# The MLP's second layers of chunks 1 to 3 as pairs of seven half products, with weight sums made by accumulating transfers

## The chip, the cores and the metric

The kernel runs on one core of a Trainium2 chip. The metric is the time of one execution in microseconds of device time, given as the median of several runs. A core has five engines that run in parallel, each in its own order: PE (matrix products; its weight loads are listed apart as PEld), DVE (elementwise work on vectors), ACT (activation functions and copies), POOL (a second elementwise engine, which also issues transfers) and SP (issues transfers). Weights and activations lie in SBUF, matrix results in PSUM, which has eight banks. Transfers between HBM and SBUF run on 16 DMA engines.

## The reference, cut to what matters

One layer of a diffusion backbone: two attention mixers, then an MLP with squared ReLU, then a last RMS norm. Width 1024, MLP width 4096, 640 tokens (128 of context, 512 latent).

```python
def _mlp(h, w_mlp_in, w_mlp_out):
    return jnp.square(jax.nn.relu(h @ w_mlp_in)) @ w_mlp_out
...
    h2 = _rmsnorm(x, n2) * (1 + sc2) + sh2
    return x + g2 * _mlp(h2, w1, w2)
...
y_prompt = _rmsnorm(xp, final_norm_g)
y_sample = _rmsnorm(xs, final_norm_g)
```

The scale, shift and gate vectors (`sc2`, `sh2`, `g2`) differ for context and latent tokens.

## The kernel before

Activations are held transposed: a tile has 128 features on the partitions and 640 tokens, in two halves of 320 (`HALVES`; `L0` and `L1` are the same). All values are f32. A product is made of three matmuls: each operand x is split into a high part (ACT rounds it to the matmul's format, fp32r) and a low part (x minus the high part, on DVE or POOL), and high x high, high x low and low x high are summed in PSUM. A full product of one output tile and one half takes 8 slices of depth x 3 = 24 matmuls of 320 columns (`gemm_k`, lines 364 to 370).

The MLP goes in four chunks of 1024 hidden features (the loop at line 1331). Each chunk has a first layer (weights `w1`, input `H2`, the normed residual) and a second (weights `w2`, input the chunk's `hid`), whose result is gated and added into the residual `X1` (`add_gated`, line 1199: one DVE instruction for half 1, two for half 0, since the gate changes at token 128). Chunk 0 is plain: 8 tiles x 2 halves of full products for each layer.

The first layers of chunks 1 to 3 already go by Winograd's form of Strassen's method (`winograd`, line 1306): a pair of output tiles and two halves of the tokens form a 2 x 2 block matrix, and so do the depths (slices 0 to 3 and 4 to 7). Seven half products of 4 slices x 3 = 12 matmuls (`product`, line 1289) replace eight. They need sums of weight blocks (S1 to S4, formed on DVE in `Weights.block`, line 268, recorded at line 278), sums of input blocks (the tiles `T` and the second half of `H2`, formed in `t_pieces`, line 1260, during chunk 0's second layer) and sums of results (DVE adds in `winograd`, line 1311). `relu2` (line 1239) then takes ReLU, square and the high part on ACT, and the low part on DVE. The second layers are full products: 8 tiles x 2 halves x 24 matmuls. The matmuls of pairs are recorded at lines 1293 to 1295, full ones at 368 to 370.

Weights: `Weights` loads tiles of 512 KB through SP into two staging buffers `st` (and two `st2` for the second tile of a pair), converts them (ACT copies the high part, lines 298 and 321; DVE or POOL subtracts for the low part, lines 299, 324 and 326) into six buffers, and converts ahead as these come free. The blocks A12 and A22 have their low part on POOL (`BLKP`), and two of the eight `w2` tiles of a chunk (`W2P`).

PSUM banks rotate through `Units` (seven of the eight); each product or half tile takes the next one. An automatic planner puts each engine's instructions in order and places the waits; it takes the written order as the priority and simulates when each is ready. For DVE alone the written order is kept from line 1128 on (`manual_schedule`). Pieces of other work are hung between products in the list `side`.

In chunk 3 each finished half of `X1` is squared and summed, then scaled by the last norm's gain; after the last half come two matmuls with `ones`, Ln and Exp on ACT, eight products and eight output transfers (`norm_pieces`, `final`).

## Time and profile before

| What | us |
|---|---|
| median of 3 runs | 968.26 (967.52 to 969.08) |
| profiled execution | 968.9 |
| its span, first to last instruction | 967.0 |
| PE busy | 943.8 |
| DVE busy | 647.8 |
| ACT busy | 504.7 |
| POOL busy | 181.0 |

The profile is that of one execution. A busy PE is not PE at its peak, since matmuls are pipelined and one recorded duration (0.309 us) covers more than the distance to the next start. Idle time of an engine that is not the bottleneck costs nothing. Of the 64 weight transfers named `wst<-w` each brings 512 KB. The first layers of chunks 1, 2 and 3 begin at about 640, 746 and 851 us, and the last matmul of chunk 3 starts at 956.80 us; the stretches quoted later follow these borders roughly.

### The profile page before, as it was taken

The page shows a single profiled execution, that of the slowest core. Times are in us where ns is not written, and L with a number is a line of the kernel's source. Part 1 is how long each engine was busy: PE and PEld are TensorE (multiplying, and loading weights), DVE is VectorE, ACT ScalarE, POOL GpSimd, SP SyncE. Part 2 cuts the span into 40 slices and gives each one's busy share as a digit, 9 for nine tenths or more (in the row PEclk, how much of TensorE's full clock was granted, in tenths as well). Part 3 has the DMA queues.
Part 4 walks back from the last instruction along what each step waited for, and adds up shares of the span by engine and source line. Part 5 has one row for each costly group of instructions (what it writes and reads, how often), then busy time and mean ns, then how long its engine had stood idle before and what let it go on. Part 6 is the DMA issues. An engine that isn't in the chain of part 4 may idle for free.

```text
span 967.0 us, 16441 instructions
## 1 busy us (share of the span) xinstructions
PE 943.8 (98%) x6375; PEld 910.2 (94%) x6375; DVE 647.8 (67%) x1336; ACT 504.7 (52%) x1061; POOL 181.0 (19%) x187
## 2 busy tenths in 40 slices
PE   8999899999999999999999999999999999999996
PEld 7799789889999999999999899999999999999995
DVE  4564766755646789698587687688734883478644
ACT  5466667656656754754324653246612762156542
POOL 0362521314321101111123000012201230022100
PEclk9999999999999999999999999999999999999998
DMA  9963310126535346466642063212321233122203
GB/s 344 230 203 110 85 44 25 27 84 150 150 91 153 109 155 218 154 196 199 202 131 88 23 184 122 66 45 88 109 88 39 86 110 94 44 88 66 88 22 109
DMA packets 35774, 111.75 MB, mean 116 GB/s; under 512 B 4672, under 2 KB 8384, under 8 KB 35696
## 3 DMA queue, kind: packets, MB, share of 16 engines
q1 hardware_dynamic: 27408, 83.49, 28.2%
q0 software_dynamic: 7136, 25.90, 9.4%
q10 hardware_dynamic: 1152, 1.31, 0.4%
q8 instruction: 50, 0.82, 0.4%
q14 instruction: 28, 0.23, 0.1%
HBM read 99.40 MB, written 4.60 MB: 108 GB/s over the span
## 4 chain that ended last, share of the span: by engine, by line
PE 85%; DVE 6%; ACT 4%; DMA 2%; issue 2%; POOL 1%; SPq 0%; DVEq 0%; ACTq 0%
PE pg L368 9%; PE pg L369 8%; PE pg L370 8%; PE pss L368 7%; PE pss L370 7%; PE pss L369 7%; PE pt L370 4%; PE pt L368 4%; PE pt L369 4%; PE pss L1293 2%; PE pss L1295 2%; PE pss L1294 2%; DMA ms<-wmodA 2%; PE pt L1293 1%; PE pg L1293 1%
## 5 line engine op out<-in xcount | busy, mean ns | idle before, releaser
L321 ACT ACTIVATE wh<-wst 128x512 fp32r<-128x512 f32 (+1 forms) x115 | 92.3, 822 | 116.4 <-PE pg L369 44.4
L326 DVE TENSOR_TENSOR wl<-wst,wh 128x1024 fp32r<-128x1024 f32 x54 | 66.0, 1222 | 63.5 <-ACT wh L321 63.3
L324 POOL TENSOR_TENSOR wl<-wst,wh 128x512 fp32r<-128x512 f32 (+1 forms) x49 | 76.5, 1575 | 136.1 <-ACT wh L321 119.5
L1083 DVE SCALAR_TENSOR_TENSOR mt<-wmt,cb 128x512 f32<-128x512 f32 x128 | 81.3, 684 | 0.0
L299 POOL TENSOR_TENSOR wb<-wst,wb 128x512 fp32r<-128x512 f32 x24 | 31.7, 1320 | 261.6 <-ACT wb L298 224.9
L644 DVE TENSOR_TENSOR pl<-pt,ph 128x512 fp32r<-128x512 f32 (+2 forms) x80 | 50.8, 635 | 36.3 <-ACT ph L643 31.4
L370 PE MATMUL pss<-hidh,wl 128*128 128x320 f32 x216 | 66.7, 309 | 0.0
L368 PE MATMUL pss<-hidh,wh 128*128 128x320 f32 x216 | 66.7, 309 | 0.0
L369 PE MATMUL pss<-hidl,wh 128*128 128x320 f32 x216 | 66.7, 309 | 0.0
L298 ACT ACTIVATE wb<-sr 128x512 fp32r<-128x512 f32 x48 | 29.8, 626 | 51.2 <-DVE sr L278 39.3
L643 ACT ACTIVATE ph<-pt 128x512 fp32r<-128x512 f32 (+2 forms) x80 | 44.2, 552 | 23.1 <-PE pt L705 10.3
L1252 DVE TENSOR_TENSOR hidl<-rl,hidh 128x320 fp32r<-128x320 f32 x64 | 36.6, 572 | 18.0 <-ACT hidh L1245 17.3
L1079 POOL DMA_DIRECT2D wmt<-wmodB x32 | 17.1, 536 | 165.6 <-DVE mt L1083 108.7
L299 DVE TENSOR_TENSOR wb<-sr,wb 128x512 fp32r<-128x512 f32 x48 | 36.0, 754 | 13.9 <-ACT wb L298 13.8
L368 PE MATMUL pg<-hidh,wh 128*128 128x320 f32 x144 | 44.5, 309 | 0.0
L369 PE MATMUL pg<-hidl,wh 128*128 128x320 f32 x144 | 44.5, 309 | 0.0
L370 PE MATMUL pg<-hidh,wl 128*128 128x320 f32 x144 | 44.5, 309 | 0.0
L368 PE MATMUL pt<-hidh,wh 128*128 128x320 f32 x136 | 42.0, 309 | 0.0
L369 PE MATMUL pt<-hidl,wh 128*128 128x320 f32 x136 | 42.0, 309 | 0.0
L370 PE MATMUL pt<-hidh,wl 128*128 128x320 f32 x136 | 42.0, 309 | 0.0
L370 PEld LDWEIGHTS pss<-hidh,wl 128*128 128x128 f32 x216 | 40.6, 188 | 0.0
L369 PEld LDWEIGHTS pss<-hidl,wh 128*128 128x128 f32 x216 | 40.6, 188 | 0.0
(950 smaller groups left out, 3362.2 us busy)
## 6 DMA issues: line engine op xcount, KB each, us to landing
wst<-w SPq DMA_DIRECT2D x64, 512.0 KB, 3.6
wmt<-wmodB POOLq DMA_DIRECT2D x32, 512.0 KB, 4.4
wst<-w_in SPq DMA_DIRECT2D x31, 512.0 KB, 3.9
ms<-wmodA SPq DMA_DIRECT2D x16, 512.0 KB, 8.0
x<-xT SPq DMA_DIRECT2D x16, 320.0 KB, 6.3
bt<-bias SPq DMA_DIRECT2D x16, 320.0 KB, 5.8
wst<-w_br SPq DMA_DIRECT2D x8, 512.0 KB, 4.5
wst<-w_out SPq DMA_DIRECT2D x8, 512.0 KB, 3.6
```

The costliest lines, as they stand in the source:

```text
L299: later.append(lambda: (nc.gpsimd if name in BLKP else DVE).tensor_sub(t[:, hi4], src, r32(t[:, lo4])))
L321: ACT.activation(hi[:, ks], st[:, ks], AF.Copy)
L324: nc.gpsimd.tensor_sub(lo[:, ks], st[:, ks], r32(hi[:, ks]))
L326: DVE.tensor_sub(lo, st, r32(hi))
L368: PE.matmul(ps, wh[:, k], xh[:, sl], start=first, stop=False)
L369: PE.matmul(ps, wh[:, k], xl[:, sl], start=False, stop=False)
L370: PE.matmul(ps, wl[:, k], xh[:, sl], start=False, stop=last)
L643: ACT.activation(ph[:, :n], pt[:, :n], AF.Copy)
L644: DVE.tensor_sub(pl[:, :n], pt[:, :n], r32(ph[:, :n]))
L1083: DVE.scalar_tensor_tensor(t, st[:, q * 512:(q + 1) * 512], 1.0, r32(cb[2 * q + i][:, :512]), op0=OP.mult, op1=OP.mult, accum_out=parts[:, ...
L1252: DVE.tensor_sub(dst[1][:, sl], r[:, :HT], r32(dst[0][:, sl]))
L1293: PE.matmul(ps, w[:, k], xh, start=k == 0, stop=False)
```

## The change

The second layers of chunks 1 to 3 become pairs of seven half products too. A pair is the output tiles 2n and 2n + 1. For this the host puts the hidden features of these chunks in another order (`w2` in `_host`), so that the first layer's four groups of results are the four blocks of the second layer's input: 11, 12, 21 and 22. `SEQ` lists all products of both layers of the three chunks; the end of a first layer and the begin of its second are interwoven (`FIRST1`, `FIRST2`).

The hidden results stay unsplit in four tiles of 4 x 320 (`hid_raw`), and `relu2r` makes them by two ACT steps. `t_raw` forms the sums T3, T2, T4 and T1 in place on DVE; `operand` splits B11, B21, T3, T4, T2, T1 and the negative of block 22 into a high and a low part of 4 x 320 each, in three rotating buffers. Signs are chosen so that weights need only be added.

Weight sums leave DVE. Of a pair, the first tile goes to a staging buffer A (three, shared with `Weights`), the second to a buffer B (four). A transfer issued on POOL's queue adds half of the first tile onto half of B while it lands (`accum_op`), which makes S3; after a block is converted, further transfers add the next part in place and make S2, S4 and S1. All weight blocks have their low part on DVE, but for A12 and A22 of the first layers on POOL.

All eight banks serve as one pool. A12's product adds into the bank of A11, S1's and S4's into that of S2. Products are gated from their bank straight into `X1` (`gate_half`); in chunks 1 and 2 the sum of A11 and S3, which two results share, is kept and added into `X1` in the next chunk's first layer (`fold`). In chunk 3 it is added at once. From there on DVE's order too is the planner's (`AUTO`). The last norm of half 0 starts while products of half 1 still run. The ring memory for transfers issued by POOL is set to 8192.

Cut to its core (the removed functions stand in the code above):

```diff
+NST = 3
+NB = 4
+NU = 6
+BLKPOOL = (("A12", "A22"), ())
+AUTO = 1
+LAG3 = 5
+SQP = 0
+FINP = ()
...
+        for n in range(KT):
+            yield ("w1", n), w1[n]
+        for n in range(KT):
+            yield ("w2", n), w2[0, n]
...
             DVE.tensor_sub(raw[0][:, L1], raw[1][:, L0], raw[2][:, L1])
             cut(H2[k], raw[0][:, L1], L1, L1)
+            for t in H2[k + 4]:
+                ACT.activation(t[:, L1], r32(t[:, L1]), AF.Copy, scale=-1.0)
...
+    FIRST1 = [("A11", 0), ("A22", 0), ("S3", 0), ("S3", 1), ("A22", 1), ("A12", 0), ("A11", 1), ("S2", 0), ("A12", 1),
+              ("S1", 0), ("S2", 1), ("S3", 2), ("S4", 0), ("A22", 2), ("S1", 1), ("A11", 2), ("S4", 1), ("A12", 2),
+              ("S2", 2), ("S3", 3), ("S1", 2), ("A22", 3), ("A11", 3), ("S4", 2), ("A12", 3), ("S2", 3)]
+    FIRST2 = [("A11", 0), ("S1", 3, 1), ("A11", 1), ("S4", 3, 1), ("A12", 0), ("A12", 1),
+              ("A11", 2), ("A11", 3), ("A12", 2), ("A12", 3)]
+    def products():
+        for c in range(1, 4):
+            for o, n in FIRST1:
+                yield 1, c, n, o
+            for x in FIRST2:
+                yield (1 if len(x) > 2 else 2), c, x[1], x[0]
+            for o in ("S3", "A22", "S2", "S1", "S4"):
+                for n in range(4):
+                    yield 2, c, n, o
+    SEQ = list(products())
...
+    class Operands:
...
+        def src(self, l, c, n, e):
+            return (w1[8 * c + 2 * n + e] if l == 1 else w2[c, 2 * n + e]).rearrange("p (k n) -> p k n", k=KT)
+        def feed(self):
+            while self.nl < len(self.loads):
+                l, c, n, x = self.loads[self.nl]
+                if x == "A":
+                    if W.nd < len(W.order) or W.busy + self.busy["A"] >= NST:
+                        return
+                    t = wp.tile([P, KT, P], F32, tag="st", bufs=NST, name="wst")
+                else:
+                    if self.busy["B"] >= NB:
+                        return
+                    t = bp.tile([P, KT, P], F32, tag="sb", bufs=NB, name="wsb")
+                nc.sync.dma_start(t, self.src(l, c, n, x == "B"))
+                self.st[l, c, n, x] = t
+                if x == "B":
+                    nc.gpsimd.dma_start(t[:, 0:4], self.src(l, c, n, 0)[:, 0:4], accum_op=OP.add)
+                self.busy[x] += 1
+                self.nl += 1
...
+        def conv(self):
+            self.feed()
+            l, c, n, o = SEQ[self.nc]
+            k = (l, c, n, "A" if o in ("A11", "A12") else "B")
+            t = self.st[k]
+            t = t[:, 0:4] if o in ("A11", "S3", "S2", "S4") else t[:, 4:8]
+            w = wp.tile([P, KT, P], F32R, tag="w" + "hl"[self.nc % 2], bufs=3, name="wb")
+            ACT.activation(w[:, 0:4], t, AF.Copy)
+            (nc.gpsimd if o in BLKPOOL[l - 1] else DVE).tensor_sub(w[:, 4:8], t, r32(w[:, 0:4]))
+            if o in ("S3", "S2", "A22"):
+                e, half = {"S3": (1, 1), "S2": (0, 1), "A22": (1, 0)}[o]
+                nc.gpsimd.dma_start(t, self.src(l, c, n, e)[:, 4 * half:4 * half + 4], accum_op=OP.add)
+            elif o in ("A12", "S4"):
+                self.free(*k)
+            self.t[SEQ[self.nc]] = w
+            W.live += 1
+            self.nc += 1
+            self.feed()
+        def ahead(self):
+            self.feed()
+            while self.nc < len(SEQ) and W.live < 6 and (SEQ[self.nc][0], *SEQ[self.nc][1:3],
+                                                         "A" if SEQ[self.nc][3] in ("A11", "A12") else "B") in self.st:
+                self.conv()
...
+    if AUTO:
+        manual.close()
+    v_pool.close()
+    m = ctx.enter_context(tc.tile_pool(name="ops", bufs=1, side="right", reuse_waits="tile"))
+    banks.close()
+    pp8 = ctx.enter_context(tc.tile_pool(name="pp8", bufs=1, space=bass.MemoryType.PSUM, reuse_waits="tile"))
+    neg = parts[:, 1]
+    DVE.tensor_scalar(neg[:, 24:32], mods[:, 24:32], -1.0, None, op0=OP.mult)
+    def bank():
+        return pp8.tile([P, 512], F32, tag="b", bufs=8, name="b")[:, :HT]
...
+    XOF = {"A11": "B11", "A12": "B21", "S3": "T3", "S2": "T2", "A22": "T4", "S1": "T1", "S4": "N22"}
+    XN = {"A11": natural(0, L0), "A12": natural(4, L0), "S3": formed(3), "S2": formed(2), "A22": natural(0, L1),
+          "S1": formed(1), "S4": natural(4, L1)}
...
+    def opd(c, name):
...
+        return OPD[c, name]
+    def hid_raw(c, b):
+        if (c, b) not in HID:
+            HID[c, b] = m.tile([P, 4, HT], F32, tag=f"hid{b}", bufs=1, name=f"hid{b}")
+        return HID[c, b]
+    def operand(c, name, ks=slice(0, 4)):
+        t, src = opd(c, name), hid_raw(c, {"B11": 11, "B21": 21, "T4": 21, "N22": 22}.get(name, 12))[:, ks]
+        hi, lo = t[:, ks], t[:, 4 + ks.start:4 + ks.stop]
+        if name == "N22":
+            ACT.activation(hi, src, AF.Copy, scale=-1.0)
+            DVE.scalar_tensor_tensor(lo, src, -1.0, r32(hi), op0=OP.mult, op1=OP.subtract)
         else:
+            ACT.activation(hi, src, AF.Copy)
+            DVE.tensor_sub(lo, src, r32(hi))
+    def t_raw(c, name, ks=slice(0, 4)):
+        b11, b12, b21, b22 = (hid_raw(c, b)[:, ks] for b in (11, 12, 21, 22))
+        if name == "T3":
+            DVE.tensor_sub(b12, b22, b12)
+        elif name == "T2":
+            DVE.tensor_add(b12, b12, b11)
+        elif name == "T4":
+            DVE.tensor_sub(b21, b21, b12)
+        else:
+            DVE.tensor_sub(b12, b22, b12)
+    def relu2r(dst, src):
+        ACT.activation(dst, src, AF.Relu)
+        ACT.activation(dst, dst, AF.Square)
+    def layer1(c, n, o, b, p):
+        if o == "A11":
+            p.pv, p.w, p.x = tp1.get(), tp1.get(), tp2.get()
+            ACT.activation(p.pv, b, AF.Copy)
+        if o == "A12":
+            relu2r(hid_raw(c, 11)[:, n], b)
+        if o in ("A11", "S3") and hasattr(p, "bA11") and hasattr(p, "bS3"):
+            DVE.tensor_add(p.w, p.pv, p.bS3)
+            if hasattr(p, "bA22"):
+                DVE.tensor_sub(p.x, p.bA22, p.w)
+        if o == "S2":
+            DVE.tensor_add(p.x, p.x, b)
+            relu2r(hid_raw(c, 21)[:, n], p.x)
+        if o == "S1":
+            DVE.tensor_sub(p.w, b, p.w)
+            relu2r(hid_raw(c, 22)[:, n], p.w)
+        if o == "S4":
+            DVE.tensor_sub(p.pv, p.pv, b)
+            relu2r(hid_raw(c, 12)[:, n], p.pv)
...
+    def gate_half(i, src, h, g=None):
+        g = (mods if g is None else g)[:, 24 + i]
+        off = HALVES[h].start
+        for sl, j in SEGS[h]:
+            DVE.scalar_tensor_tensor(X1[i][:, sl], src[:, sl.start - off:sl.stop - off], g[:, j:j + 1],
+                                     X1[i][:, sl], op0=OP.mult, op1=OP.add)
...
+    def done_half(i, h):
+        x, first_, last_ = X1[i][:, HALVES[h]], not nrm[h], len(nrm[h]) == KT - 1
+        if first_:
+            nrm[h].append(tt_tile("acc3"))
+        else:
+            nrm[h].append(None)
+        acc = r32(nrm[h][0][:, L0])
+        q = acc if first_ else r32(tt_tile("sq3")[:, L0])
+        ACT.activation(q, x, AF.Square)
+        if not first_ and not last_:
+            (nc.gpsimd if SQP else DVE).tensor_add(acc, acc, q)
+        ACT.activation(x, x, AF.Copy, scale=gn[:, 2, i:i + 1])
+        if last_:
+            rs = r32(tt_tile("rstd3")[:, L0])
+            def norm():
+                b = bank()
+                PE.matmul(b, ones, acc, start=True, stop=False)
+                PE.matmul(b, ones, q, start=False, stop=True)
+                ACT.activation(rs, b, AF.Ln, bias=eps)
+                ACT.activation(rs, rs, AF.Exp, scale=-0.5)
+            def final(f):
+                y = X1[f][:, HALVES[h]]
+                (DVE if h or f not in FINP else nc.gpsimd).tensor_mul(y, y, rs)
+                (nc.sync, nc.scalar)[f % 2].dma_start(yT[:, f, HALVES[h]], y)
+            side.extend([lambda: None] * (0 if h else LAG3) + [norm] + [lambda f=f: final(f) for f in range(KT)])
...
+    WS = [None] * 4
+    def fold(n):
+        for h in range(2):
+            gate_half(2 * n + 1, WS[n], h, neg)
+    def layer2(c, n, o, b, p):
+        if c < 3:
+            if o == "A11":
+                WS[n] = tp1.get()
+                ACT.activation(WS[n], b, AF.Copy)
+                gate_half(2 * n, b, 1)
+            elif o == "S3":
+                DVE.tensor_add(WS[n], WS[n], b)
+            else:
+                e, h = {"A12": (0, 0), "A22": (1, 0), "S2": (1, 0), "S1": (1, 1), "S4": (0, 1)}[o]
+                gate_half(2 * n + e, b, h, neg if o == "S4" else None)
+            return
+        if o == "A11":
+            p.pv = tp1.get()
+            ACT.activation(p.pv, b, AF.Copy)
+            gate_half(2 * n, b, 1)
+        if o == "A12":
+            gate_half(2 * n, b, 0)
+            done_half(2 * n, 0)
+        if o == "S3":
+            DVE.tensor_add(p.pv, p.pv, b)
+        if o == "A22":
+            p.x = tp2.get()
+            DVE.tensor_sub(p.x, b, p.pv)
+            gate_half(2 * n + 1, p.pv, 1, neg)
+        if o == "S2":
+            DVE.tensor_add(p.x, p.x, b)
+            gate_half(2 * n + 1, p.x, 0)
+            done_half(2 * n + 1, 0)
+        if o == "S1":
+            gate_half(2 * n + 1, b, 1)
+            done_half(2 * n + 1, 1)
+        if o == "S4":
+            gate_half(2 * n, b, 1, neg)
+            done_half(2 * n, 1)
+    OPS[0].ahead()
+    for x in SEQ:
+        l, c, n, o = x
+        w = OPS[0].get(x)
+        if l == 1:
+            xk = XN[o]
+        else:
+            s = opd(c, XOF[o])
+            xk = lambda k, s=s: (s[:, k], s[:, 4 + k])
+        p = pairs.setdefault((l, c, n), Pair())
+        whole = {"A12": "A11", "S1": "S2", "S4": "S2"}.get(o)
+        b = getattr(p, "b" + whole) if whole else bank()
+        setattr(p, "b" + o, b)
+        for k in range(4):
+            xh, xl = xk(k)
+            PE.matmul(b, w[:, k], xh, start=not whole and k == 0, stop=False, skip_group_check=True)
+            PE.matmul(b, w[:, k], xl, start=False, stop=False, skip_group_check=True)
+            PE.matmul(b, w[:, 4 + k], xh, start=False, stop=o not in ("A11", "S2", "S1") and k == 3, skip_group_check=True)
+        (layer1 if l == 1 else layer2)(c, n, o, b, p)
+        W.live -= 1
+        if l == 1 and o in ("A12", "S2") and n > 1:
+            operand(c, "B11" if o == "A12" else "B21", slice(0, 3) if n == 2 else slice(3, 4))
+        if l == 1 and c > 1 and o == "S2":
+            fold(n)
+        if l == 1 and o == "S4" and n > 1:
+            t_raw(c, "T3", slice(0, 3) if n == 2 else slice(3, 4))
+        if l == 2:
+            if (o, n) == ("A11", 2):
+                operand(c, "T3")
+                t_raw(c, "T2")
+                t_raw(c, "T4")
+            if (o, n) == ("A11", 3):
+                operand(c, "T4")
+            if (o, n) == ("A12", 3):
+                operand(c, "T2")
+                t_raw(c, "T1")
+            if (o, n) == ("S3", 3):
+                operand(c, "T1")
+            if (o, n) == ("S2", 3):
+                operand(c, "N22")
+        OPS[0].ahead()
+        if side:
+            side.pop(0)()
...
+    w2 = np.concatenate([w2[:1], w2[1:].reshape(3, 4, 2, P, 1024).transpose(0, 2, 1, 3, 4).reshape(3, 1024, 1024)])
...
-    nc = _bacc.Bacc("TRN2", target_bir_lowering=False, num_devices=1)
+    nc = _bacc.Bacc("TRN2", target_bir_lowering=False, num_devices=1, dynamic_dma_scratch_size=8192)
```

More of the change, by code (lines that the diff above doesn't have):

```diff
@@ L43 @@
 Q0P = 0
-PLAIN = (0,)
-SUMP = ()
-BLKP = ('A12', 'A22')
 RL = 1
@@ L234, in __init__ @@
             self.pos = {k: i for i, (k, _) in enumerate(self.order)}
-            self.loads = []
-            for key, src in self.order:
-                if key[0] in BLOCKS:
-                    if src is not None and key[0] == "A11":
-                        self.loads += [((key[1], e), src[e], e) for e in range(2)]
-                else:
-                    self.loads.append((key, src, 1 if key in SECOND else 0))
-            self.st, self.t, self.raw = {}, {}, {}
-            self.nd = self.nc = self.live = self.nb = 0
@@ new lines, in __init__ @@
+            self.st, self.t = {}, {}
+            self.nd = self.nc = self.live = self.busy = 0
+            self.extra = False
+        def feed(self):
+            while self.nd < len(self.order) and self.busy < NST:
+                key, src = self.order[self.nd]
+                self.st[key] = st = wp.tile([P, KT, P], F32, tag="st", bufs=NST, name="wst")
+                nc.sync.dma_start(st, src.rearrange("p (k n) -> p k n", k=KT))
+                self.busy += 1
+                self.nd += 1
@@ L342, in done @@
             else:
-                self.live -= 1 if key and key[0] in BLOCKS else 2
+                self.live -= 2
             self.ahead()
@@ L1126, in trunk_layer @@
     un = Units()
+    manual = ExitStack()
+    ctx.callback(manual.close)
     if MAN:
-        ctx.enter_context(tc.manual_schedule(engines={(DVE.engine, ACT.engine, PE.engine)[i] for i in MAN}))
+        manual.enter_context(tc.manual_schedule(engines={(DVE.engine, ACT.engine, PE.engine)[i] for i in MAN}))
     AOS, BOS = [], []
@@ new lines, in trunk_layer @@
+    hid = [(v_tile("hidh"), v_tile("hidl")) for _ in range(KT)]
+    Wt = {}
+    for n in range(3):
+        Wt[n] = W.get("w1", n)
+    first = units([(Wt[n], 0) for n in range(3)], H2, 6)
+    for n, h in [(i, h) for h in range(2) for i in range(4)] + [(i, h) for i in range(4, KT) for h in range(2)]:
+        if n not in Wt:
+            Wt[n] = W.get("w1", n)
+        ps = first.pop(0) if first else unit(Wt[n], H2, h)
+        if h:
+            W.done("w1", n)
+        relu2(hid[n], ps, h)
+        flush_later(posts)
+        if not side:
+            mod_pace(1600)
@@ new lines, in trunk_layer, with __init__, free, get @@
+    class Operands:
+        def __init__(self):
+            self.st = {}
+            self.loads = []
+            for l, c, n, o in SEQ:
+                k = (l, c, n, "A" if o in ("A11", "A12") else "B")
+                if k not in self.loads:
+                    self.loads.append(k)
+            self.t = {}
+            self.nl = self.nc = 0
+            self.busy = {"A": 0, "B": 0}
+        def src(self, l, c, n, e):
[17 more added lines that the diff above has]
+                self.nl += 1
+        def free(self, *k):
+            del self.st[k]
+            self.busy[k[3]] -= 1
+        def conv(self):
+            self.feed()
+            l, c, n, o = SEQ[self.nc]
+            k = (l, c, n, "A" if o in ("A11", "A12") else "B")
+            t = self.st[k]
[17 more added lines that the diff above has]
+                self.conv()
+        def get(self, x):
+            while x not in self.t:
+                self.conv()
+            return self.t.pop(x)
@@ new lines, in trunk_layer @@
+    OPS.append(Operands())
+    Wt = {n: W.get("w2", n) for n in range(2)}
+    first = units([(Wt[n], 0) for n in range(2)], hid, 6)
+    for n, h in [(0, 0), (1, 0), (0, 1), (1, 1)] + order(KT, 0)[4:]:
+        if n not in Wt:
+            Wt[n] = W.get("w2", n)
+        ps = first.pop(0) if first else unit(Wt[n], hid, h)
+        if h:
+            W.done("w2", n)
+        add_gated(n, ps, h, 3)
+    while side:
+        side.pop(0)()
+    flush_later()
+    if AUTO:
+        manual.close()
```

209 lines of the change are left out of this document (45 added, 164 removed).

## The prediction

> **What bounds the kernel now.** I read the page first (busy shares, the chain that ended last), then busy time by stretch, then who waited for whom on TensorE, then the groups by line with each form apart.
>
> ```profile
> span 967.0 us, 16441 instructions
> ...
> PE 85%; DVE 6%; ACT 4%; DMA 2%; issue 2%; POOL 1%; SPq 0%; DVEq 0%; ACTq 0%
> ```
> ```profile
> 500.00:560.00 60.00, 58.54 (x385) 56.53 (x384) 43.81 (x98) 29.90 (x66) 8.89 (x6) 1.00 0.23 68
> 560.00:956.95 396.95, 396.95 (x2705) 396.63 (x2704) 260.69 (x470) 182.70 (x346) 47.20 (x32) 1.00 0.27 83
> 956.95:967.00 10.05, 1.51 (x6) 0.49 (x4) 3.85 (x9) 2.03 (x4) 0.00 (x0) 0.74 0.37 130
> ```
> ```profile
> PE pt L192 <- ACT sq L184: 0.6, 1, 0.6
> ```
>
> The columns of the second fence are the stretch, its length, then busy time and instructions of PE, PEld, DVE, ACT and POOL, the granted clock, the DMA share and GB/s. From 560.00 to 956.95 TensorE is busy for the whole stretch at a granted clock of 1.00. The third fence is the whole list of TensorE's waits after 560 us: one of 0.6 us, in the tail. So here the end moves by what TensorE is spared, until something else becomes late. One matmul of 320 columns takes 396.95 / 2705 = 0.1467 us start to start. A half product (12 matmuls) is 1.76 us.
>
> Chunks 1 to 3 alternate between first layers (28 half products, 336 matmuls, 49.3 us) and second layers (8 tiles x 2 halves x 8 k x 3 = 384 matmuls, 56.3 us). One stretch of nearly each kind:
>
> ```profile
> 850.00:902.00 52.00, 52.00 (x356) 52.00 (x356) 43.61 (x71) 35.18 (x73) 13.96 (x9) 1.00 0.27 82
> 902.00:957.00 55.00, 55.00 (x374) 54.68 (x373) 26.71 (x54) 24.61 (x44) 0.00 (x0) 1.00 0.20 63
> ```
>
> The first layer keeps DVE busy 84%, the second 49%, with a fifth to a quarter of DMA.
>
> **What the change removes.** Each second layer of chunks 1 to 3 becomes 4 pairs x 7 half products x 12 = 336 matmuls in place of 384. The first layers keep 336. So TensorE is spared 3 x 48 = 144 matmuls, 144 x 0.1467 = **21.1 us**. Nothing hides this and nothing in the diff adds a matmul; the norm's four stay. All else is what may become late.
>
> **DVE's new load.** Rows by form (last three numbers: busy us, mean ns, idle before):
>
> ```profile
> L299 DVE TENSOR_TENSOR wb<-wst,wb 128x512 fp32r<-128x512 f32 x12 | 8.2, 684 | 0.0
> L326 DVE TENSOR_TENSOR wl<-wst,wh 128x1024 fp32r<-128x1024 f32 x23 | 28.2, 1226 | 52.1 <-ACT wh L321 51.9
> L278 DVE TENSOR_TENSOR sr<-wst,sr 128x512 f32<-128x512 f32 x12 | 14.9, 1240 | 0.0
> L278 DVE TENSOR_TENSOR sr<-sr,wst 128x512 f32<-128x512 f32 x12 | 8.3, 692 | 0.4
> L1311 DVE TENSOR_TENSOR cc<-pv,pss 128x320 f32<-128x320 f32 x20 | 9.6, 481 | 0.2
> L1202 DVE SCALAR_TENSOR_TENSOR x<-pss,parts,x 128x320 f32<-128x320 f32 x11 | 6.0, 548 | 8.8 <-PE pss L370 8.8
> L1202 DVE SCALAR_TENSOR_TENSOR x<-pss,parts,x 128x192 f32<-128x192 f32 x17 | 6.9, 407 | 0.0
> L1202 DVE SCALAR_TENSOR_TENSOR x<-pss,parts,x 128x128 f32<-128x128 f32 x17 | 5.9, 348 | 8.8 <-PE pss L370 8.8
> L186 DVE TENSOR_TENSOR acc<-acc,sq 128x320 f32<-128x320 f32 x12 | 5.9, 492 | 8.3 <-ACT sq L184 8.3
> L1236 DVE TENSOR_TENSOR x<-x,rstd 128x320 f32<-128x320 f32 x16 | 6.8, 484 | 5.7 <-ACT rstd L194 5.7
> ```
>
> An operand part has 4 x 320 = 1280 elements, which no row has; between 320 (0.484) and 1024 (1.226) the slope is 1.05 ns an element, so I estimate 1.50 us. These rows are recorded durations; back to back they cost less, as three neighbours show (0.39 and 0.40 us start to start for 0.48 recorded), so about 0.08 us less each:
>
> ```profile
> 867.48 0.48 DVE L1311 TENSOR_TENSOR cc<-pv,pss 128x320 f32<-128x320 f32 x1
> 867.87 0.48 DVE L1252 TENSOR_TENSOR hidl<-rl,hidh 128x320 fp32r<-128x320 f32 x1
> 868.27 0.68 DVE L299 TENSOR_TENSOR wb<-wst,wb 128x512 fp32r<-128x512 f32 x1
> ```
>
> Second layer of chunks 1 and 2: 28 weight remainders x 0.684 = 19.2; per pair three gates of half 0 (0.348 + 0.407 each), three of half 1 (0.548) and one add (0.481), 4.39 x 4 = 17.6; operands: five low parts and three raw sums, 8 x 1.50 = 12.0. Sum 48.8 us recorded in 76 instructions, 42.7 back to back, against 49.3 us of TensorE. It fits, nearly full.
>
> Second layer of chunk 3: the pairs cost 7.11 each (two half-0 gates, four half-1 gates, three adds, four adds of squares) less four squares adds that the first and last halves lack: 28.4 - 2.0 = 26.5; with 19.2 and 12.0, 57.7; half 0's eight last products, 3.9, make 61.6 recorded in 100 instructions, 53.6 back to back. Six blocks converted ahead (4.1) fall before it and about five of those last products (2.0 to 2.4) into the tail, where DVE is idle for 2.46 us. That leaves 47.5 to 55.1 against 49.3: a stall of **0 to 5.9 us**. I take 1.0, as the back-to-back spacing is what a loaded DVE shows.
>
> First layer: 20 remainders (13.7), 20 adds (9.6), the folds of the chunk before (4 x 1.30 = 5.2), raw T3 and two low parts (about 5): 33.4. The 16 weight sums a chunk (the L278 rows) and the 16 low parts of hid go. POOL keeps its eight subtractions, and beside those DVE's rows are slower: 1240 ns in the one L278 form against 692 in the other. If all 8 x 1.32 us were lost, 44 of 49.3 us: covered.
>
> ```profile
> L299 POOL TENSOR_TENSOR wb<-wst,wb 128x512 fp32r<-128x512 f32 x24 | 31.7, 1320 | 261.6 <-ACT wb L298 224.9
> L1079 POOL DMA_DIRECT2D wmt<-wmodB x32 | 17.1, 536 | 165.6 <-DVE mt L1083 108.7
> L298 ACT ACTIVATE wb<-wst 128x512 fp32r<-128x512 f32 x36 | 22.0, 618 | 26.6 <-issue 11.8 <-PE pt L369 8.9 <-PE pg L369 6.0
> ```
>
> ACT: 56 copies x 0.618 = 34.6 of 98.5 us a chunk, and some 30 us of relu, squares and operand copies: covered. POOL: 32 accumulating issues a chunk, x 0.536 = 17.2, and 10.6 of subtractions: covered, though a subtraction of A12 or A22 queued behind an issue that waits for its tile waits with it, and TensorE then for that block; the six blocks ahead (10.6 us) cover it.
>
> **Banks used twice.** A12 adds into A11's bank, S1 and S4 into S2's, so they must wait until ACT or DVE has read it; before, each product had a fresh bank. In the written order ten such hand-overs a chunk have one product (1.76 us) between. The trace has no such wait; the nearest is how soon a bank is read now:
>
> ```profile
> 860.69 0.31 PE L1295 MATMUL pt<-t,wb 128*128 128x320 f32 x1
> 861.45 0.48 DVE L1311 TENSOR_TENSOR cd<-cc,pt 128x320 f32<-128x320 f32 x1
> ```
>
> The product ends at 861.00 and is read by 861.93, 0.93 us later: inside 1.76. With a 1.50 us operand part in DVE's way it would be 0.67 us late. That can meet about four hand-overs a chunk, around A11 2 and A11 3 of the second layer, where four such parts are queued. Bounds 0 to, with two parts in the way (2.17 us) each time, 12 x 2.17 = 26; DVE's order is the planner's now, which may put the short gate first. I take **2.0 us** (three misses of 0.67), near the row. Operands at the layer's start: A12 3's two relu steps, copy and remainder (about 2 us) lie beside S2 3 and nine matmuls (3.1 us). Below nothing: a third staging buffer might help the 100 to 300 us stretch; I know no wait there that it ends, and allow 1 us.
>
> **The accumulating transfers.** Each B tile is loaded, then takes four transfers of 256 KB in a row, each after the block before it is converted.
>
> ```profile
> q1 hardware_dynamic: 7488, 24.38, 24.3%
> ```
> ```profile
> wmt<-wmodB POOLq DMA_DIRECT2D x32, 512.0 KB, 4.4
> wst<-w SPq DMA_DIRECT2D x64, 512.0 KB, 3.6
> silu<-sc_e POOLq DMA_DIRECT2D x2, 4.0 KB, 14.4
> ```
>
> The first row is of 640 to 967 us: 24.38 MB in 24.3% of 327 us, 307 GB/s while transferring. A chunk loads 8.39 MB and accumulates 8.39 MB: at that rate 27.3 + 27.3 = 54.6 of 98.5 us, with no loss. Landing: nearest row 4.4 us, far row 14.4. S3 to S4 of a pair are at least ten products apart in the first layer and conversion may run five ahead: 15 x 1.76 = 26.4 us for two landings and three conversions of 1.3, so up to 11 us a landing is hidden. I take 4.4: nothing.
>
> In the Trainium skill, "Collectives: The Full Stack", section "The bandwidth ceiling: the fold count and why AG ≠ RS ≠ AR", an adding transfer reads two sources on one ring and so moves at half a copy's rate. No row here can show it. By it the engines would be taken 27.3 + 54.6 = 81.9 of 98.5 us, and the sum would stand.
>
> **The tail** stays: last gate, square, two norm matmuls, Ln, Exp, eight products, out.
>
> ```profile
> 957.15 0.55 DVE L1202 SCALAR_TENSOR_TENSOR x<-pss,parts,x 128x320 f32<-128x320 f32 x1 [1.94 <-PE pss L370]
> 960.16 3.30 DVE L1236 TENSOR_TENSOR x<-x,rstd 128x320 f32<-128x320 f32 x8 [2.46 <-ACT rstd L194]
> ```
>
> **Sum.** The profiled execution took 968.9 us (span 967.0 and 1.9 around it): 968.9 - 21.1 + 1.0 + 2.0 = 950.8. The median of the runs shown is 968.26, 0.64 less: forecast **950.1 us**.
>
> **Rivals.** *DVE becomes the bound.* If a loaded DVE costs its recorded durations, chunk 3 stalls 5.9 us, and the late gates in the three second layers 2.17 us four times each time in a third of cases (8.7): 968.3 - 21.1 + 5.9 + 8.7 = about 962. For it: the sums above are nearly full. Against: the spacing, and stretches now at 84% DVE with no TensorE wait.
>
> *Slower: the accumulating transfers become the bound.* In chunks 1 to 3, if an accumulated byte takes the engines three times as long as a loaded one, a chunk needs 27.3 + 81.9 = 109.2 us against 98.5: 947.2 + 3 x 10.7 = 979. It decides from 118 GB/s accumulated (71.2 us) on, and is slower than before from 107 (105.6 - 27.3 = 78.3 us). For it: no row has an accumulation, and transfers in the trace range from 3.6 to 14.4 us. Against: 44 us of room. By the skill's half rate this rival would not occur; with that alone I would halve its chance.
>
> *No gain:* the planner's orders put so many late reads in TensorE's way that all 21.1 us go: 30 hand-overs x 0.7 us. About 968.
>
> **How the numbers follow.** Forecast (946 to 954.5) 0.57; DVE bound (954.5 to 966) 0.31; transfers 0.09, of which 0.07 above 970; no gain 0.03. The range 945.5 to 962 holds the forecast, its lower bound (947.2 less 1, and a little) and most of the second case: about 0.8. A measurement of this kernel can tell about 0.2%: faster 0.90, same 0.03, slower 0.07.
>
> **What would show it.** Right: 144 matmuls fewer; TensorE nearly full from 560 us to some 10 us before the end; its waits a few, short, on DVE gates or ACT copies of banks. DVE bound: DVE at 95% in chunk 3's second layer, gates there starting over 2 us after their product. Transfers: ACT's weight copies waiting on DMA, landings over 11 us, a DMA share near 1. Wrong altogether: TensorE idle at the layer changes, or the stretch before 560 us changed by over 1 us.

## The result, and the profile after

The changed kernel takes 950.91 us (median of four runs, 950.13 to 952.27) against 967.89 for the kernel before in the same job (four runs): ratio 0.9825, 95% interval 0.9808 to 0.9842. The forecast was 950.1, with a range of 945.5 to 962. The profiled execution took 951.01 us.

From the page of the changed kernel: the span, the busy times, the two groups in which POOL issues the adding transfers, and their time from issue to landing.

```profile
span 949.2 us, 16613 instructions
...
PE 923.6 (97%) x6231; PEld 887.5 (93%) x6231; DVE 690.0 (73%) x1401; ACT 542.9 (57%) x1120; POOL 251.7 (27%) x277
...
L1327 POOL DMA_DIRECT2D wsb<-w x72 | 63.6, 918 | 91.5 <-DVE wb L1324 63.0
...
L1308 POOL DMA_DIRECT2D wsb<-w x24 | 23.0, 960 | 90.4 <-DMA wsb<-w 70.4
...
wsb<-w POOLq DMA_DIRECT2D x96, 256.0 KB, 5.2
```

TensorE has 6375 - 6231 = 144 matmuls fewer, as counted. The spans differ by 17.8 us, and 144 x 0.1467 is 21.1, so some 3.5 us were given back. To say where, the changed stretch must be taken by itself: ahead of it, where the kernels are the same, single executions come to differ by some 3 us in the first 160 us, and by less than 0.1 us more from there to 530 us. A mark is the first matmul on block 6 of `H2` in chunk 0's first layer, which both kernels have (timeline: start, duration, engine, line). Here are its rows, first of before, then of after.

```profile
531.69 0.31 PE L368 MATMUL pg<-hh6h,wh 128*128 128x320 f32 x1
```
```profile
531.35 0.31 PE L300 MATMUL pg<-hh6h,wh 128*128 128x320 f32 x1
```

From the mark to the end of the span: 967.0 - 531.69 = 435.31 us before and 949.2 - 531.35 = 417.85 after, 17.46 less. With all 21.1 us gained it would be 414.2, so **3.6 us** were given back behind the mark. All waits of TensorE from 560 us on (total, times, longest) and the timeline of the largest stop at a layer's start show most of them; between the mark and 560 us both kernels have the same one wait of 1.4 us, at a norm.

```profile
PE b L1478 <- DVE acc L1471: 0.5, 1, 0.5
PE b L1548 <- DVE op L1412: 0.4, 1, 0.4
PE b L1479 <- ACT sq L1469: 0.4, 2, 0.2
```
```profile
686.13 0.31 PE L1547 MATMUL b<-op,wb 128*128 128x320 f32 x1
686.83 0.42 PE L1548 MATMUL b<-op,wb 128*128 128x320 f32 x1 [0.40 <-DVE op L1412]
```

From 686.13 to 686.83 is 0.70 us in place of 0.1467, and the next start comes 0.10 late too: 0.65 us lost at this layer's start. Measured in the same way, start to start, the three second layers lose 0.65, 0.37 and 0.40 = 1.4 us at their start, where the last slice of an operand is late, and 0.13, 0.38 and 0.32 = 0.8 us where A12 3 takes the bank of A11 3 (half product and pair). One block of weights comes 0.3 late. The norm in the middle of chunk 3's second layer costs 0.5 more than the one in the kernel before (1.3 against 0.8). From the start of the last product's last matmul to the end of the span it is 10.71 us, before it was 10.20: 0.5 more, since the last norm waits for the last addition of squares. That makes the 3.6.

Busy time by stretch (columns as in the prediction): a second layer, a first layer, and two pieces of chunk 3's second layer.

```profile
787.00:837.00 50.00, 49.88 (x340) 49.62 (x339) 44.70 (x80) 25.93 (x41) 15.95 (x18) 1.00 0.80 166
837.00:886.00 49.00, 48.87 (x334) 48.60 (x333) 36.55 (x56) 32.26 (x65) 22.87 (x22) 1.00 0.82 174
...
906.00:926.00 20.00, 20.00 (x138) 20.00 (x137) 20.00 (x39) 12.38 (x20) 6.93 (x8) 1.00 0.72 111
926.00:934.00 8.00, 7.77 (x50) 7.00 (x49) 8.00 (x17) 5.20 (x11) 0.00 (x0) 1.00 0.01 2
```

DVE is busy 0.89 of the second layer and without a break from 906 to 934 us, but TensorE loses little there. In the first two of these stretches the DMA engines are busy for four fifths of the time; in the kernel before it was a fifth to a quarter.

### The profile page after: what moved, and what is told of

Same layout as the page of the kernel before. It is cut to its first block, busy times and chain, and to the rows that moved or that the text cites. A ratio compares the mean times of both kernels' runs of the same rounds, so it can differ in the third digit from the quotient of the medians.

```text
span 949.2 us, 16613 instructions
## 1 busy us (share of the span) xinstructions
PE 923.6 (97%) x6231; PEld 887.5 (93%) x6231; DVE 690.0 (73%) x1401; ACT 542.9 (57%) x1120; POOL 251.7 (27%) x277
## 4 chain that ended last, share of the span: by engine, by line
PE 74%; DVE 10%; DMA 5%; ACT 5%; issue 3%; POOL 1%; SPq 0%; DVEq 0%; ACTq 0%; POOLq 0%
PE b L1547 8%; PE b L1548 8%; PE b L1549 7%; PE pg L300 7%; PE pg L302 7%; PE pg L301 6%; PE pss L302 4%; PE pss L300 4%; PE pss L301 4%; DMA ms<-wmodA 3%; PE pt L302 3%; PE pt L301 3%; PE pt L300 3%; DVE wb L1324 1%; PE pt L637 1%
## 5 line engine op out<-in xcount | busy, mean ns | idle before, releaser
L1323 ACT ACTIVATE wb<-wsb 128x512 fp32r<-128x512 f32 x120 | 74.8, 628 | 75.2 <-PE b L1549 49.2
L1548 PE MATMUL b<-op,wb 128*128 128x320 f32 x336 | 104.1, 310 | 0.6 <-DVE op L1412 0.4
L1547 PE MATMUL b<-op,wb 128*128 128x320 f32 x336 | 104.2, 310 | 0.2
L1549 PE MATMUL b<-op,wb 128*128 128x320 f32 x336 | 103.8, 309 | 0.0
L1324 DVE TENSOR_TENSOR wb<-wsb,wb 128x512 fp32r<-128x512 f32 x108 | 78.7, 732 | 31.8 <-ACT wb L1323 30.2
L257 ACT ACTIVATE wh<-wst 128x512 fp32r<-128x512 f32 (+1 forms) x92 | 68.0, 765 | 57.7 <-PE pg L301 19.1
L1327 POOL DMA_DIRECT2D wsb<-w x72 | 63.6, 918 | 91.5 <-DVE wb L1324 63.0
L1548 PEld LDWEIGHTS b<-op,wb 128*128 128x128 f32 x336 | 63.1, 188 | 1.4 <-DVE op L1412 1.4
L1547 PEld LDWEIGHTS b<-op,wb 128*128 128x128 f32 x336 | 63.0, 188 | 1.1 <-DVE x L1455 1.0
L1549 PEld LDWEIGHTS b<-op,wb 128*128 128x128 f32 x336 | 63.1, 188 | 0.0
L262 DVE TENSOR_TENSOR wl<-wst,wh 128x1024 fp32r<-128x1024 f32 x37 | 45.2, 1222 | 22.0 <-ACT wh L257 22.0
L575 ACT ACTIVATE ph<-pt 128x512 fp32r<-128x512 f32 (+2 forms) x80 | 44.1, 552 | 21.7 <-PE pt L637 10.3
L1308 POOL DMA_DIRECT2D wsb<-w x24 | 23.0, 960 | 90.4 <-DMA wsb<-w 70.4
L1547 PE MATMUL b<-t,wb 128*128 128x320 f32 x144 | 44.6, 310 | 0.0
L1549 PE MATMUL b<-t,wb 128*128 128x320 f32 x144 | 44.5, 309 | 0.0
L1548 PE MATMUL b<-t,wb 128*128 128x320 f32 x144 | 44.5, 309 | 0.0
L1455 DVE SCALAR_TENSOR_TENSOR x<-b,parts,x 128x128 f32<-128x128 f32 (+1 forms) x92 | 38.3, 441 | 3.6 <-PE b L1549 1.8
L1323 ACT ACTIVATE wb<-wst 128x512 fp32r<-128x512 f32 x48 | 29.9, 626 | 15.5 <-PE b L1549 9.3
```

Source lines behind the costliest of these rows:

```text
L257: ACT.activation(hi[:, ks], st[:, ks], AF.Copy)
L1323: ACT.activation(w[:, 0:4], t, AF.Copy)
L1324: (nc.gpsimd if o in BLKPOOL[l - 1] else DVE).tensor_sub(w[:, 4:8], t, r32(w[:, 0:4]))
L1327: nc.gpsimd.dma_start(t, self.src(l, c, n, e)[:, 4 * half:4 * half + 4], accum_op=OP.add)
L1547: PE.matmul(b, w[:, k], xh, start=not whole and k == 0, stop=False, skip_group_check=True)
L1548: PE.matmul(b, w[:, k], xl, start=False, stop=False, skip_group_check=True)
```

## The experiments

Twelve kernels ran, in three jobs; the kernel before had medians of 967.70, 968.15 and 968.06 us in these. "From the mark" is the profiled execution's span less the start of the matmul named above. `c0_after` is the changed kernel again.

| kernel | median, us | ratio to before, 95% interval | from the mark, us |
|---|---|---|---|
| c0_after | 951.64 | 0.9818 to 0.9845 | 417.81 |
| e1_order | 949.63 | 0.9796 to 0.9823 | 417.35 |
| e2_written | 985.88 | 1.0153 to 1.0193 | 453.18 |
| e3_fewer | 947.72 | 0.9776 to 0.9818 | 415.37 |
| e4_plain | 948.37 | 0.9787 to 0.9814 | 415.47 |
| e5_more | 1036.55 | 1.0685 to 1.0733 | 503.62 |
| e6_pe_written | 959.27 | 0.9884 to 0.9926 | 424.82 |
| e7_pool | 957.48 | 0.9883 to 0.9916 | 426.06 |
| e9_fewer_plain | 939.04 | 0.9678 to 0.9716 | 405.04 |
| e10_dve | 947.58 | 0.9778 to 0.9810 | 415.87 |
| e14_more_plain | 964.51 | 0.9938 to 0.9975 | 426.72 |
| e15_fewer_dve | 943.82 | 0.9737 to 0.9766 | 409.39 |

**The changed kernel again** (`c0_after`, no edit).

> The changed kernel as it stands, beside the others on one chip: 949.5 to 952.5 us, the base for the differences of 1 us below.

417.81 us from the mark against 417.85: the stretch repeats to 0.04 us, though the medians differ by 0.7. Differences of a microsecond are read from this column; with one execution of each kernel, half a microsecond is near its limit. The single stops do not repeat as well as their sum: here the three layers' starts lose 0.8, 0.6 and nothing, and two blocks of weights come 0.3 late.

**Order at the end of the first layer** (`e1_order`).

```diff
-("S2", 2), ("S3", 3), ("S1", 2), ("A22", 3), ("A11", 3), ("S4", 2), ("A12", 3), ("S2", 3)]
+("S2", 2), ("S3", 3), ("A22", 3), ("A11", 3), ("S1", 2), ("A12", 3), ("S4", 2), ("S2", 3)]
```

> S1 2 and S4 2 of the first layers move behind A11 3 and A12 3, so that two products instead of one lie between A12 3 of the first layer and A11 0 of the second. Theory (at the start of each second layer TensorE waits for the last slice of operand B11, made from A12 3): the three stops there, 0.65, 0.37 and 0.40 us, go; TensorE's list of waits loses the one on the operand; 1.0 to 1.4 us less than the changed kernel. Rival (the operand part is late because DVE is full, not because A12 3 is late): the stops stay within 0.2 us of what they were and the time does not move.

All of TensorE's waits from 640 us on:

```profile
PE b L1547 <- DVE tp L1441: 0.8, 1, 0.8
PE b L1478 <- DVE acc L1471: 0.5, 1, 0.5
PE b L1479 <- ACT sq L1469: 0.4, 2, 0.2
```

The waits on the operand (L1412) are gone, so these did come from the order at the layer's end. But a stop of 0.8 us on an addition of the first layer (L1441) is new, and from the mark the gain is 0.5 us, not the 1.0 to 1.4 expected. The medians differ by 2.0; in the profiled executions 2.0 of the 2.5 us between the spans lie ahead of the mark, where the kernels are the same.

**Who sets the order** (`e2_written`: DVE kept in the written order; `e6_pe_written`: TensorE kept in it, DVE left to the planner).

```diff
-AUTO = 1
+AUTO = 0
```
```diff
     if AUTO:
         manual.close()
+    ctx.enter_context(tc.manual_schedule(engines={PE.engine}))
```

> DVE keeps the written order to the end instead of the planner's. Theory (the planner's order puts short gates ahead of the long operand parts, which is why the hand-overs of banks cost only 0.8 us): with the written order the gate of A11 3 stands behind T3's low part and two raw sums (4.4 us), and each of three layers loses 2 to 4 us: 955 to 965 us, with TensorE's waits on DVE gates in front. Rival (order does not matter, as DVE has room): within 1 us of the changed kernel.

> TensorE keeps the written order in chunks 1 to 3, DVE's order is the planner's. In the changed kernel the planner has put S3 0 and S3 1 of the second layer between A12 2 and A12 3. Theory (that is what hides the hand-over of A11 3's bank): with the written order A12 3 waits for a gate behind long operand parts, 1 to 3 us in each of three layers, 954 to 960 us. Rival (the gate is read in time anyway): within 1 us of the changed kernel.

TensorE's longest waits from 640 us on, first of `e2_written`, then of `e6_pe_written` (its lines are one higher: L1456 is the gate):

```profile
PE b L1547 <- DVE tp L1441: 6.6, 5, 2.2
PE b L1547 <- ACT op L1411: 3.9, 2, 2.1
PE b L1547 <- ACT wb L1323: 3.7, 5, 0.9
PE b L1547 <- DVE x L1455: 3.5, 6, 1.4
```
```profile
PE b L1548 <- DVE x L1456: 6.0, 5, 1.8
```

With DVE in the written order it takes 35 us more, with late additions, operands, weights and gates. That is far above the 955 to 965 us expected, and not from the gates alone. With TensorE in the written order it takes 7 us more, within what was expected and nearly all of it gates: the hand-over from A11 3 to A12 3 loses 2.0 us in each second layer. In the changed kernel the planner puts S3 0 and S3 1 between A12 2 and A12 3, and the loss is 0.1 to 0.4.

**The additions of squares on POOL** (`e7_pool`).

```diff
-SQP = 0
+SQP = 1
-FINP = ()
+FINP = tuple(range(8))
```

> Sums of squares of the last norm (12 adds) and half 0's eight last products go from DVE to POOL. Theory (DVE is full in chunk 3's second layer but late for almost nothing that TensorE needs, so only the late norm of half 0, about 0.4 us, and a longer tail, about 0.5 us, can be won): 0 to 1.0 us less than the changed kernel. Rival (DVE is the bound of that layer): it does 9 us less work there, and 3 us or more are won. A third case: POOL's own adds are slower than DVE's and the last sum comes late, up to 1 us more.

```profile
PE b L1478 <- POOL acc L1471: 4.0, 1, 4.0
PE b L1547 <- ACT x L1472: 1.7, 1, 1.7
```

These are TensorE's two longest waits. A miss: 8.2 us slower from the mark, 5.8 in the medians. To take work off a DVE that is busy without a break did not help; the last norm then waits 4.0 us for POOL, whose last addition of squares (at 943.25) stands behind four of half 0's products (3.31 us from 939.98 on).

**Plain transfers** (`e4_plain`), the same bytes without the addition, so that the weight sums are left out.

```diff
-nc.gpsimd.dma_start(t[:, 0:4], self.src(l, c, n, 0)[:, 0:4], accum_op=OP.add)
+nc.gpsimd.dma_start(t[:, 0:4], self.src(l, c, n, 0)[:, 0:4])
-nc.gpsimd.dma_start(t, self.src(l, c, n, e)[:, 4 * half:4 * half + 4], accum_op=OP.add)
+nc.gpsimd.dma_start(t, self.src(l, c, n, e)[:, 4 * half:4 * half + 4])
```

> The 96 transfers that add onto a B tile write over it instead, so the weight sums are left out; sizes, queue and order stay. Theory (accumulation is hidden): the DMA share of chunks 1 to 3 falls from 0.79 to about 0.5 and the landing from 5.2 to about 4.4 us, but the time stays within 0.5 us of the changed kernel (only a stop of 0.3 us at 673 us can go). Rival (late weight blocks cost most of what was lost between 560 and 940 us): 1.5 to 2.7 us less.

The queue of these transfers from 640 us on (packets, MB, share of the engines' time), first in the changed kernel, over 309.2 us, then here, over 306.6 us, with the landing:

```profile
q0 software_dynamic: 12816, 23.34, 48.8%
```
```profile
q0 software_dynamic: 7120, 23.34, 24.1%
...
wsb<-w POOLq DMA_DIRECT2D x89, 256.0 KB, 3.3
```

23.34 MB in 48.8% of 309.2 us is 155 GB/s; plain, in 24.1% of 306.6 us, 316 GB/s. An adding transfer takes the engines twice as long and lands in 5.2 us in place of 3.3. The addition costs the kernel 2.3 us from the mark (3.3 in the medians): the theory said 0.5 at most, and the 2.3 lie in the rival's range. Only the waits for squares are left to TensorE. That the cost came through late weight blocks alone, as the rival had it, isn't shown: the stops that went are for the most part on operands and banks, and POOL's issues became shorter too (544 ns in place of 918).

**Some transfers twice**, adding (`e5_more`) and plain (`e14_more_plain`, with the first one of each tile plain too). Two of the four transfers of a B tile are doubled; in the first kernel the weight sums hold a term twice, in the second they are left out.

```diff
-nc.gpsimd.dma_start(t, self.src(l, c, n, e)[:, 4 * half:4 * half + 4], accum_op=OP.add)
+for _ in range(2 if o in ("S3", "S2") else 1):
+    nc.gpsimd.dma_start(t, self.src(l, c, n, e)[:, 4 * half:4 * half + 4], accum_op=OP.add)
```

> Two of the four accumulating transfers of each B tile are issued twice (48 more of 256 KB, 12.6 MB; the sums then hold a term twice). Measured rates: 155 GB/s accumulating, 307 GB/s plain. Theory (throughput decides, from the point where a chunk's transfers need more than its 98.5 us): 12.6 MB x 1/155 + 8.4 MB x 1/307 = 81 + 27 = 108 us a chunk, a DMA share near 1 and about 20 to 30 us more, 970 to 980. Rival (there is more room than the shares show): within 3 us of the changed kernel. Second rival (the longer chain of landings decides, 10 us for each doubled step): TensorE waits at single blocks, with a DMA share well below 1.

> Plain transfers (both additions left out), and the second and third load of each weight pair issued twice, as in the run that measured 1036.6 with adding transfers. Theory A: what counts is the chain of landings behind each conversion and POOL's line, which must stay under some 5 us per step: two plain landings take about 6.6 us in place of 5.2, over 48 steps, so part of 67 us comes: 960 to 985. Rival B: what counts is the bytes over the time of the DMA engines: those of the doubled plain loads keep the engines no busier than the single adding ones did (0.8), so 948 to 953.

POOL's longest wait from 640 us on, in `e5_more` and in `e14_more_plain` (L1328 is the issue), and one stretch of `e5_more`:

```profile
POOL wsb L1328 <- DMA wsb<-w: 113.5, 38, 7.4
```
```profile
POOL wsb L1328 <- DMA wsb<-w: 56.5, 33, 4.3
```
```profile
640.00:690.00 50.00, 41.19 (x251) 40.66 (x250) 22.95 (x31) 23.94 (x46) 24.32 (x24) 0.90 0.77 153
```

POOL issues in order: the second transfer waits until the first has landed, and all that POOL has behind it waits too. Adding, that costs 86 us from the mark, far more than expected; plain, 11 us against `e4_plain`, as its theory A said. In `e5_more` TensorE is busy for 41 of 50 us at a DMA share of 0.77, no more than in the changed kernel (0.80); later stretches of 90 us have 0.79 and 0.87. So it is the time from step to step that counts, nearest to the second rival, and not the engines' capacity. From an issue to its landing it is 3.3 us plain and 5.2 adding; for a doubled step I estimate twice the landing, 6.6 plain and 11 adding. With these the kernel takes 415.5, 417.8, 426.7 and 503.6 us: the price starts below 5.2 us and rises steeply. How much is the landing and how much POOL's line wasn't separated. A part of the rise is TensorE's clock: behind the mark 169 matmuls of `e5_more` start 0.24 to 0.31 us apart in place of 0.147, which adds 20 us; in the changed kernel 12 do, 1.3 us. The granted clock of 0.90 in the stretch above shows the same.

**Fewer products** (`e3_fewer`), to see what comes next behind TensorE; `e9_fewer_plain` is the same with plain transfers, `e15_fewer_dve` the same with POOL's weight subtractions of the first layers on DVE.

```diff
+            if k != 1:
-            PE.matmul(b, w[:, k], xl, start=False, stop=False, skip_group_check=True)
+                PE.matmul(b, w[:, k], xl, start=False, stop=False, skip_group_check=True)
```
```diff
-BLKPOOL = (("A12", "A22"), ())
+BLKPOOL = ((), ())
```

> One of the twelve matmuls of each half product is left out in chunks 1 to 3 (high weights by low input of slice 1): 168 matmuls, 24.6 us of TensorE at 0.1467, with all work of the other engines kept. Theory (TensorE still bounds all but chunk 3's second layer, where DVE is full): 20 to 22 us less than the changed kernel, about 930, the 4.1 us of chunk 3's second layer (28 matmuls) not won. Rival 1 (TensorE bounds everywhere, DVE has room): 24 us less, about 926.5. Rival 2 (DVE is the bound in all second layers): the 12.3 us of these are not won, about 938.

> As the run with fewer products, which leaves out one matmul in 24 of chunks 1 to 3 (24.6 us of TensorE) and measured 947.7, but the weight sums are transferred plainly: both additions by transfer are left out too. Theory A: what took the place of the 24.6 us there is the chain of adding transfers that land in 5.2 us and are issued in order by POOL. Then plain ones, which land in 3.3, give most of it back: 948.4 (plain transfers alone) less 20 to 24.6, so 924 to 929. Rival B: VectorE's gates and the conversions bind, and the transfers take no part: only the 3.3 us come off that plain transfers gave before, so 943 to 946.

> Leaves out the same one matmul in 24 (24.6 us), and POOL's weight subtractions of the first layers go to VectorE; transfers add as in the change. Against 947.7 with the subtractions on POOL. Theory A (the delays that POOL's subtractions cause to VectorE and to the transfers behind them are a large part of what took the 24.6 us): 932 to 942. Rival B (the landings themselves, or VectorE's sum): 946 to 951.

TensorE's two longest waits in `e3_fewer`, and one stop with what follows it (timeline, then the granted clock, third from the end, in the stretches around it):

```profile
PE b L1547 <- DVE tp L1441: 5.1, 2, 3.2
PE b L1550 <- DVE wb L1324: 4.6, 4, 2.4
```
```profile
747.05 0.31 PE L1550 MATMUL b<-hh7h,wb 128*128 128x320 f32 x1
750.52 0.63 PE L1547 MATMUL b<-t,wb 128*128 128x320 f32 x1 [3.17 <-DVE tp L1441]
750.95 0.47 PE L1549 MATMUL b<-t,wb 128*128 128x320 f32 x1
751.22 0.47 PE L1550 MATMUL b<-t,wb 128*128 128x320 f32 x1
```
```profile
750.50:753.00 2.50, 2.48 (x9) 2.48 (x10) 0.65 (x1) 2.14 (x5) 1.44 (x2) 0.50 0.72 125
```

Of 24.6 us taken from TensorE, 2.4 are gained from the mark (417.81 to 415.37); all three expected times (926.5 to 938) were missed. So behind TensorE the change has left other limits, some 2 us away. About 5 us of the loss are the slow matmuls after stops (56 starts 0.24 to 0.31 us apart, 10 in `c0_after`). With plain transfers 10.3 us more come out, with the subtractions on DVE 6.0. Each lies between its theory A and its rival: `e9_fewer_plain` gives 939.0 where A said 924 to 929 and B 943 to 946, `e15_fewer_dve` 943.8 where A said 932 to 942 and B 946 to 951. So the transfers and POOL's subtractions each take part, and neither is all of it. In `e9_fewer_plain` 14 of the 24.6 us are still lost against `e4_plain`, 4 of them in slow matmuls after stops. DVE's additions of the first layer (L1441) are 5.0 us late there, at two places, and ahead of both DVE works without a break for over 16 us (729.47 to 746.28 and 824.89 to 841.71), on gates, subtractions and additions: there it is VectorE's load that holds TensorE, as the rival had it. The other stops weren't traced.

**The first layers' subtractions on DVE, with e1's order** (`e10_dve`): the diffs of `e1_order` and `BLKPOOL` together.

> The changed order of the first layer's last steps (949.6 by itself), and the eight weight subtractions that POOL does for each chunk's first layer go to VectorE. Theory A: a POOL subtraction costs VectorE more than it spares: gates from SBUF to SBUF beside it took 2.06 us in place of 0.35, and POOL's transfers stand in line behind it. Then VectorE's sum stays about the same (plus 8 times 0.69, less about three delays of 1.7 for each chunk), the transfers go out earlier and TensorE's lost gaps fall by a part of the 2.1 us: 948.0 to 949.4. Rival B: VectorE, at 0.9 of the second layers, is what is short, and the gates of the layer before run later: 950 to 953.

DVE's groups of the gate (busy us, mean ns, idle before), with the page's line of busy times, first of `c0_after`, then of `e10_dve`:

```profile
PE 924.0 (97%) x6231; PEld 888.2 (93%) x6231; DVE 689.0 (72%) x1401; ACT 543.7 (57%) x1120; POOL 252.1 (27%) x277
...
L1455 DVE SCALAR_TENSOR_TENSOR x<-b,parts,x 128x128 f32<-128x128 f32 (+1 forms) x92 | 38.4, 443 | 3.6 <-PE b L1549 1.8 <-ACT tp L1500 1.0 <-ACT tp L1510 0.5
...
L1455 DVE SCALAR_TENSOR_TENSOR x<-tp,parts,x 128x128 f32<-128x128 f32 (+2 forms) x36 | 22.4, 662 | 0.0
```
```profile
PE 921.3 (97%) x6231; PEld 887.1 (94%) x6231; DVE 690.3 (73%) x1425; ACT 544.4 (58%) x1120; POOL 217.9 (23%) x253
...
L1455 DVE SCALAR_TENSOR_TENSOR x<-b,parts,x 128x128 f32<-128x128 f32 (+1 forms) x92 | 38.5, 444 | 5.2 <-PE b L1549 2.1 <-ACT tp L1500 1.7 <-ACT tp L1510 0.8
...
L1455 DVE SCALAR_TENSOR_TENSOR x<-tp,parts,x 128x128 f32<-128x128 f32 (+2 forms) x36 | 14.3, 436 | 0.0
```

DVE takes 24 subtractions more, 24 x 0.69 = 16.6 us, and its busy time grows by 1.3 (by 0.7 against `e1_order`, which has the same order): so POOL's 24 subtractions had cost DVE about 15 us. The gates whose operands all lie in SBUF (`x<-tp,parts,x`) take 436 ns in place of 662, those that read a bank (`x<-b,parts,x`) are unchanged. The Trainium skill, "SBUF — State Buffer", section "SBUF: two separate sides", has this: VectorE and GpSimd share a pair of ports as an exclusive lock, which a VectorE instruction with two SBUF inputs needs against a GpSimd one that reads SBUF; the rows agree.

Theory A holds, and the time comes out a little below its 948.0 to 949.4. From the mark the kernel is 1.9 us faster than the change and 1.5 faster than with the order alone, and from 640 us to the last norm no wait of TensorE on an operand, a weight or a bank is left. At 947.58 us (947.21 to 949.71, five runs) it is the fastest of those that compute the whole layer: its interval lies below that of `c0_after`.

## Why the prediction was right

The forecast was 950.1, the median 950.91. From the mark the sum said -21.1 + 1.0 + 2.0 = -18.1 us; measured are -17.5. Point by point:

- **144 matmuls, 21.1 us.** The count is right and the price holds: TensorE still starts a matmul every 0.147 us where it doesn't wait. The experiment `e10_dve`, with nearly all stops gone, comes within 1.7 us of the full gain (415.87 against 414.2).
- **DVE, 1.0 us (0 to 5.9).** DVE was as full as worked out: busy 94% of chunk 3's second layer (886 to 938.5 us), 28 us of it without a break, and an operand part took 1.48 us where 1.50 was estimated. TensorE lost about 0.5 there at the norm in the middle. The rival "DVE becomes the bound" had its load right; the late gates that it priced at 8.7 us cost 0.8 (the next point), since the planner set the order. `e2_written` shows the price without that: 35 us in all, more than the upper bounds of this and the next term together (31.9).
- **Banks used twice, 2.0 us (0 to 26).** 0.8 us, at one place in each second layer. The row-based miss of 0.67 was about right in kind, and the bound of two parts in the way (2.17) is what `e6_pe_written` shows when TensorE keeps the written order (2.0 each).
- **The operand at the layer's start, 0.** This step failed, by 1.4 us. I took nine matmuls and S2 3 as cover for A12 3's steps. The timeline has ACT's and DVE's conversions of weights between those steps (DVE's subtraction of 0.68 us at 685.29 and the addition at 685.89 stand right ahead of the operand's last slice, L1412), and nothing in my 2 us counted them. `e1_order` gave the steps more room, and the waits went; with plain transfers in the old order they went too (`e4_plain`), so either is enough. The prediction had named TensorE idle at the layer changes as a sign of being wrong; it came, at this small size.
- **Adding transfers, 0.** The second step that failed, by 2.3 us. I estimated a landing of 4.4 us and a price only from 11 us on; it was 5.2, and `e4_plain`, `e14_more_plain` and `e5_more` show that the price starts below 5.2 us. The cover of "up to 11 us" counted the pair's own steps alone, not POOL's line, in which each issue takes 0.92 us (0.54 was taken from a plain one). The 2.3 us are no sum beside the stops above but overlap with them, as plain transfers end those too; by which path an adding transfer delays operands and gates stays open.
- **Adding transfers as the bound** (979, chance 0.09) did not occur. The rate was 155 GB/s, above the 118 from which it decides: a chunk takes 27.3 + 8.39 MB / 155 GB/s = 81 us of the engines. The Trainium skill's half rate, from "Collectives: The Full Stack", section "The bandwidth ceiling: the fold count and why AG ≠ RS ≠ AR", gave 81.9; the trace agrees, 155 against 316 GB/s. The Trainium skill has this for the adding step of a ReduceScatter.
- **POOL's subtractions.** I priced them at 8 x 1.32 us of DVE a chunk and held them covered. They cost about 15 / 3 = 5 us a chunk; with more room in order that is worth 1.5 us here (`e10_dve`).
- **The tail, 0.** It is 0.5 us longer. The last norm's first matmul starts 0.65 us late for the last addition of squares: its gate is done at 937.63, its square starts on ACT at 938.22, behind steps of half 0's norm and a scaling, and the addition follows at 938.75.

So the large term, the matmuls, was right in mechanism and size, and TensorE stayed the bound as forecast. The sizes of the small terms were off in both directions, and it is luck that they balanced to 0.6 us: 3.0 us priced at two places, 3.6 paid at five.

## What to carry to other kernels

Where TensorE is busy throughout, a removed matmul is worth its start-to-start time until the next limit, so ask how far that limit is: here a further 24.6 us off TensorE gained 2.4. A chain of transfers that each wait for the one before is hidden by what really stands between two steps on every queue involved, the issuing engine's line among them, not by the products alone. And compare small changes over a stretch that both kernels have, from a common mark, for executions differ elsewhere by more than such a change is worth.

## What the runs showed of the hardware

- While they kept the DMA engines busy, transfers that add into SBUF moved 155 GB/s where plain ones moved 316. An adding one landed in 5.2 us in place of 3.3, and its issue took POOL 0.92 us in place of 0.54.
- After a stop of 3.2 us (`e3_fewer`) TensorE ran at a granted clock of 0.50 for the next 2.5 us: matmuls started 0.27 us apart in place of 0.147. It was the same after a stop of 2.5 us in `e9_fewer_plain` (0.50 from 746.3 to 748.8), and after one of the three stops of 1.8 us in `e6_pe_written` (0.50 from 905 to 908, 0.7 us after work began again). So a longer stop is paid more than once; the stop of 0.4 us in the changed kernel shows no such stretch.
- A subtraction on POOL cost DVE 0.6 us on average, almost as much as doing it (0.69).
